# Where streamed and stationary operands begin in memory: a float32 decoder on one core

## The chip, the cores and the metric

The kernel runs on one core of a Trainium2 chip. The core has a matrix engine, TensorE (PE in the profile; its weight loads are listed apart, as PEld), two engines for elementwise work, VectorE (DVE) and ScalarE (ACT), a small helper, GpSimd (POOL), and queues that move data from the chip's main memory, HBM, into the on-chip memory, SBUF. SBUF has 128 partitions; a tile has a row in each. TensorE takes two operands from SBUF: the *stationary* one, 128 columns that a weight load puts into the array, and the *streamed* one, up to 512 columns that then pass through it. The products are summed in a third memory, PSUM.

The metric is the time of one execution in microseconds (us), the median of several.

## The reference

Two decoder layers and a final norm, on 256 tokens of width 1024, in float32:

```python
for l in range(DEPTH):                       # 2
    h = rmsnorm(x, norm1[l])
    hq, hf, hi, hg, aq, ak, av, ga, gb = split_cols(h @ w_in[l])     # 1024 -> 7680 columns
    o_hg = hgrn2_chunked(silu(hq), 1 - f, hi, log(f))               # f from sigmoid(hf); 8 heads of 128
    y_a = (rmsnorm(o_hg, hg_norm[l]) * silu(hg)) @ w_pa[l]
    y_b = swa_with_sinks(rope(aq), rope(ak), av, attn_sinks[l]) @ w_pb[l]   # window 128, 16 / 4 heads of 64
    x = x + (sigmoid(ga) * y_a + sigmoid(gb) * y_b) @ w_o[l]
    h2 = rmsnorm(x, norm2[l])
    x = x + (silu(h2 @ w_gate[l]) * (h2 @ w_up[l])) @ w_down[l]     # hidden width 2816
return rmsnorm(x, final_norm)
```

The weights of the two layers are about 159 MB and are read once.

## The kernel before

**Three products for one.** TensorE's quick float32 mode rounds its operands, so each operand is split into a rounded high part and a rest, and three of the four cross products are summed. For a weight tile `raw` from HBM, ScalarE rounds it into `wh` and VectorE subtracts to get `wl` (function `ahead`, 300 pairs of 128 x 1024 elements). The activations are split in the same way, into `xh` and `xl`, `ah` and `al`, and so on.

**Two forms.** In form A (`form_a`, `down`) the activations are stationary, 128 tokens at a time, and the weights are streamed, 512 columns at a time: `ah` with `wh`, `ah` with `wl`, `al` with `wh`. The products `akv`, `aq`, `v`, `gate`, `gb`, `ga`, `yb`, `ya`, `wo` and `acc` (the product with `w_down`) are of this form, with 2160 streams of 512 columns in all. In form B (`form_b`) the weights are stationary, 128 columns at a time, and the activations are streamed. There `xx` holds the high and the low part side by side, 256 tokens each:

```python
self.xx = hp.tile([P, KT, 2, S], F32R, tag="xx", name=f"xx_{name}")
T.matmul(ps, wh[:, k, :], n.xx[:, k], start=k == 0, stop=k == KT - 1)               # wide: 512 columns
T.matmul(ps[:, 0:S], wl[:, k, :], n.xx[:, k, 0, :], start=False, stop=False)        # narrow: 256 columns
```

So a *wide* stream takes `wh` against both parts, and a *narrow* one `wl` against the high part. They come four and four: wide, narrow, narrow, wide, for the eight k tiles of a product. `pb` (the columns for `hf` and `hq`), `pg` (`w_gate`) and `pu` (`w_up`) are of this form. `pb` streams the activations of the first norm, `n1`, whose tile is also the stationary operand of `akv`, `aq`, `v`, `gate`, `gb` and `ga`; `pg` and `pu` stream those of the second norm, `n2`, which nothing else uses.

Every stream has a weight load of its own, of 128 columns, and the load for the next stream goes on beside the one that runs.

**Order.** The large products run one after the other on TensorE, in the order `akv`, `aq`, `v`, `pb`, `gate`, `gb`, `yb`, `ga`, `ya`, `wo`, and then groups of `pg`, `pu` and `acc`. The small products of attention and of the recurrence (`qk`, `pt`, `pv`, `lb`, `lv`, `lc`, `o`, ...) are side work, put between them by generators. The weights run ahead of their use: three raw tiles and five pairs of `wh` and `wl` are held, and ScalarE and VectorE refill a pair when TensorE is through with it.

**Where the tiles lie.** Within a partition, every tile that TensorE reads begins at a multiple of 64 bytes, and a row of 512, 256 or 128 elements of 4 bytes is a multiple of 64 too. So both operands of each of its instructions begin there.

All engine calls go through one helper, so that the profile puts them on line 55 and tells them apart by their tiles (`out<-in`).

Of the kernel before, what the change touches and what calls it, by code (L numbers as in the profile page):

```python
# [8 lines left out]
F32R = mybir.dt.float32r  # L9
# [6 lines left out]
P = 128  # L16
D = 1024
S = 256
NT = S // P
DEPTH = 2  # L20
KT = D // P
# [6 lines left out]
EPS = 1e-6  # L28
MIN_F = 1e-30
NRAW, NW = 3, 5  # L30
YA, YB, YC, YS, YO, YP, YD, YE, YQ = 4, 3, 4, 2, 2, 2, 3, 2, 5
NEG = -1e30

# [7 lines left out]
def trunk(ctx, tc, x, norm1, w_in, lb_logits, hg_norm, attn_sinks, w_pa, w_pb, w_o, norm2,  # L41
# [4 lines left out]
    class Ordered:  # L46
        def __init__(self, engine):
            self.engine = engine
            self.always = engine is nc.tensor
# [11 lines left out]

    hp = ctx.enter_context(tc.tile_pool(name="hp", bufs=1))
    hp.tile([P, 224], F32, tag="lead", name="lead")
    hp.tile([P, KT, 2, S], F32R, tag="xx", name="xx_lead")
    st = hp.tile([P, 8, P], F32, tag="st", name="st")
    cp = ctx.enter_context(tc.tile_pool(name="cp", bufs=1))
    rawp = ctx.enter_context(tc.tile_pool(name="rawp", bufs=NRAW))
    wp = ctx.enter_context(tc.tile_pool(name="wp", bufs=NW))
# [34 lines left out]
    g2, ghg, lbl = (gcol[:, i, 0] for i in range(3))  # L103
# [56 lines left out]
                plan += [(w_down[l], groups[gi - 1][0], 4, 512 * c, 512) for c in range(2)]  # L160
        plan.append((w_down[l], groups[-1][0], 2, 0, D))

    raws, ready = [], []
    taken = [0]

    def load(j):
        src, k0, nk, c0, n = plan[j]
        raw = rawp.tile([P, nk, n], F32, tag="raw", name=f"raw{j}")
        step_ = nk // 2 if j < 2 else nk
        for k in range(0, nk, step_):  # L170
            nc.sync.dma_start(raw[:, k:k + step_], src[(k0 + k) * P:(k0 + k + step_) * P, c0:c0 + n].rearrange(
                "(k p) c -> p k c", p=P))
        if j == 0:
            nc.sync.dma_start(xs[1], x[0, P:2 * P, :])
        elif j == 1:
            nc.sync.dma_start(cf, const_f)
            G.memset(rows, 0.0)
            for i, vec in enumerate((norm2, hg_norm, lb_logits)):
                nc.scalar.dma_start(rows[32 * i:32 * i + 16, :], vec.rearrange("l (k p) -> (l k) p", p=P))
            nc.scalar.dma_start(nsink, attn_sinks.rearrange("l h -> (l h)").partition_broadcast(P))  # L180
        if nk == KT:
            parts = [raw[:, :, i * P:(i + 1) * P] for i in range(n // P)]
        elif n == 512:
            parts = [raw[:, 2 * i:2 * i + 2, :] for i in range(nk // 2)]
        else:
            parts = [raw[:, i:i + 1, :] for i in range(nk)]
        raws.extend(parts)
# [3 lines left out]
    def ahead(n):  # L191
        while len(ready) < min(n, 2 * len(plan)):
            while loaded[0] < len(plan) and len(raws) < len(ready) + 4:
                load(loaded[0])
                loaded[0] += 1
            i = len(ready)
            shape = list(raws[i].shape)
            hi = wp.tile(shape, F32R, tag="wh", name=f"wh{i}")
            lo = wp.tile(shape, F32R, tag="wl", name=f"wl{i}")
            A.copy(hi, raws[i])  # L200
            V.tensor_tensor(lo, raws[i], hi.bitcast(F32), ALU.subtract)
            ready.append((hi, lo))

    def take(n):
        i = taken[0]
        ahead(i + max(n, NW - 1))
        taken[0] += n
        return ready[i:i + n]

    def used():  # L210
        done[0] += 1
        ahead(done[0] + NW - 1)
# [65 lines left out]
        A.activation(dst, ps, AF.Copy, scale=r)  # L278

    class Norm:  # L280
        def __init__(self, gain, name):
            self.gain, self.name = gain, name
            self.xx = hp.tile([P, KT, 2, S], F32R, tag="xx", name=f"xx_{name}")
            self.xh, self.xl = self.xx[:, :, 0, :], self.xx[:, :, 1, :]
            self.rb = sm.tile([P, 1, S], F32, tag="rb", name=f"rb_{name}", bufs=1)
            self.ss = sm.tile([P, NT, 3], F32, tag="ss", name=f"ss_{name}")
            self.r = [sm.tile([P, 1], F32, tag=f"r{t}", name=f"r_{name}{t}") for t in range(NT)]
# [79 lines left out]
    def layer(l, n1):  # L367
# [422 lines left out]
        for _ in it:  # L790
            pass

        n2 = Norm(g2[:, l], f"n2_{l}")
        parts = []

        def put_x(c):
# [132 lines left out]
    nx = Norm(g1[:, 0], "n1_0")  # L929
    nx.turn(0, 0)  # L930
    ahead(1)
    nx.turn(0, 1)
    ahead(2)
# [19 lines left out]
    for l in range(DEPTH):  # L953
        hold = []

        def whole():
            hold.append((yield from layer(l, nx)))

        run(whole())
        nx = hold[0]  # L960
# [53 lines left out]
```

## Time and profile before

| what | before |
|---|---|
| median of 3 runs | 948.55 us (948.11 to 948.85) |
| the profiled execution | 948.29 us, of it 946.6 us from the first to the last instruction |
| granted TensorE clock, mean | 0.997 |
| TensorE busy, matmuls | 931.1 us in 5706 |
| TensorE weight loads | 777.8 us in 5706 |
| VectorE, ScalarE busy | 678.4 us, 538.0 us |
| DMA | 161.13 MB, 170 GB/s |

A group row of the profile gives line, engine, operation and tiles, the shapes, the count, the busy time in us and the mean duration of one in ns, then the engine's idle time just before them and what ended it. A matmul's duration runs from its start to a modelled end, which lies well behind the next one's start, since the matmuls are pipelined. What a matmul takes from TensorE's time is the distance to the next start, and this is read from the pieces of the chain of waits, or from starts in the timeline.

### The profile page before, as it was taken

The numbers are of one execution on the slowest core, as the hardware profiler recorded it, in microseconds if no ns is written. First come the engines' busy times: TensorE is split into PE (matmuls) and PEld (weight loads), VectorE is DVE, ScalarE is ACT, GpSimd is POOL, SyncE is SP. The second block draws the span as 40 slices with busy tenths as digits, with TensorE's granted clock in tenths as the row PEclk, the third lists the DMA queues.
The fourth block names the chain that finished last, engine by engine and source line by source line (L and its number), as shares of the span: only waits on it lengthen the run. The fifth ranks groups of instructions, "written<-read, shape, count | busy, mean of one in ns | idle before, by whom it ended". The sixth has DMA issues, their size and how long they took to land.

```text
span 946.6 us, 14348 instructions
## 1 busy us (share of the span) xinstructions
PE 931.1 (98%) x5706; PEld 777.8 (82%) x5706; DVE 678.4 (72%) x1176; ACT 538.0 (57%) x914; POOL 16.4 (2%) x28
## 2 busy tenths in 40 slices
PE   7999999999999999999999999999999999999996
PEld 5878887888888888888878888878788888888885
DVE  6567879976677867766585677898857787667664
ACT  6556596545446555554465776955454555455543
POOL 1000000000000000000000000000000000000000
PEclk9999999999999999999999999999999999999998
DMA  7645454444455566556466444554445566556541
GB/s 284 224 129 176 142 167 138 168 144 153 159 176 179 179 188 207 183 180 201 152 201 200 134 134 134 178 179 135 144 157 180 166 198 200 180 180 203 195 135 45
DMA packets 110932, 161.13 MB, mean 170 GB/s; under 512 B 2769, under 2 KB 64401, under 8 KB 110865
## 3 DMA queue, kind: packets, MB, share of 16 engines
q1 hardware_dynamic: 110160, 159.12, 51.7%
q10 hardware_dynamic: 704, 1.10, 0.3%
q8 instruction: 45, 0.74, 0.3%
q14 instruction: 23, 0.18, 0.1%
HBM read 159.15 MB, written 1.05 MB: 169 GB/s over the span
## 4 chain that ended last, share of the span: by engine, by line
PE 94%; ACT 2%; DVE 2%; DMA 0%; issue 0%; POOL 0%; POOLq 0%; ACTq 0%; SPq 0%
PE pg L55 13%; PE pu L55 13%; PE acc L55 12%; PE pb L55 8%; PE yb L55 5%; PE ga L55 5%; PE gb L55 5%; PE gate L55 5%; PE wo L55 5%; PE ya L55 5%; PE aq L55 5%; PE v L55 4%; PE akv L55 2%; PE qk L55 1%; PE o L55 1%; PE pv L55 1%
## 5 line engine op out<-in xcount | busy, mean ns | idle before, releaser
L55 DVE TENSOR_TENSOR wl<-raw,wh 128x1024 fp32r<-128x1024 f32 x300 | 365.8, 1223 | 146.2 <-ACT wh L55 144.4
L55 ACT CAST wh<-raw 128x1024 fp32r<-128x1024 f32 x300 | 314.9, 1053 | 203.6 <-PE acc L55 61.3
L55 PE MATMUL pu<-xx_n,wh 128*128 128x512 f32 x352 | 92.6, 393 | 0.0
L55 PE MATMUL pg<-xx_n,wh 128*128 128x512 f32 x352 | 92.5, 393 | 0.0
L55 PEld LDWEIGHTS pg<-xx_n,wh 128*128 128x128 f32 x352 | 63.2, 189 | 10.9
L55 PEld LDWEIGHTS pu<-xx_n,wh 128*128 128x128 f32 x352 | 63.1, 189 | 10.9
L55 PE MATMUL acc<-wl,ah 128*128 128x512 f32 x176 | 69.0, 392 | 0.0
L55 PE MATMUL acc<-wh,al 128*128 128x512 f32 x176 | 68.8, 391 | 0.0
L55 PE MATMUL acc<-wh,ah 128*128 128x512 f32 x176 | 68.2, 391 | 0.0
L55 PE MATMUL pb<-xx_n,wh 128*128 128x512 f32 x256 | 67.3, 397 | 0.0
L55 PEld LDWEIGHTS pb<-xx_n,wh 128*128 128x128 f32 x256 | 45.1, 189 | 8.8 <-issue 1.0
L55 PEld LDWEIGHTS pu<-xx_n,wl 128*128 128x128 f32 x352 | 48.4, 190 | 3.6
L55 PEld LDWEIGHTS pg<-xx_n,wl 128*128 128x128 f32 x352 | 48.1, 190 | 3.9 <-ACT xx_n L55 0.6
L55 PE MATMUL pg<-xx_n,wl 128*128 128x256 f32 x352 | 50.1, 284 | 0.0
L55 PE MATMUL pu<-xx_n,wl 128*128 128x256 f32 x352 | 49.7, 282 | 0.0
L55 ACT COPY zg<-pg 128x256 f32<-128x256 f32 x44 | 16.4, 373 | 54.1 <-PE pg L55 54.1
L55 PE MATMUL ga<-wh,xx_n 128*128 128x512 f32 x128 | 43.7, 402 | 0.0
L55 PE MATMUL gb<-wh,xx_n 128*128 128x512 f32 x128 | 43.1, 400 | 0.0
L55 PE MATMUL v<-wh,xx_n 128*128 128x512 f32 x128 | 41.2, 395 | 0.0
L55 PE MATMUL gate<-wh,xx_n 128*128 128x512 f32 x128 | 40.9, 394 | 0.0
L55 PE MATMUL aq<-wh,xx_n 128*128 128x512 f32 x128 | 40.3, 391 | 0.0
L55 ACT ACTIVATE sp<-sp,stat 128x128 f32<-128x128 f32 (+1 forms) x64 | 28.3, 443 | 19.8 <-DVE stat L55 19.8
(221 smaller groups left out, 1671.7 us busy)
## 6 DMA issues: line engine op xcount, KB each, us to landing
raw<-in_w_in SPq DMA_DIRECT2D x58, 1024.0 KB, 5.2
raw<-in_w_gate SPq DMA_DIRECT2D x22, 1024.0 KB, 5.1
raw<-in_w_up SPq DMA_DIRECT2D x22, 1024.0 KB, 5.2
raw<-in_w_down SPq DMA_DIRECT2D x22, 1024.0 KB, 5.0
raw<-in_w_pb SPq DMA_DIRECT2D x8, 1024.0 KB, 5.0
raw<-in_w_pa SPq DMA_DIRECT2D x8, 1024.0 KB, 5.2
raw<-in_w_o SPq DMA_DIRECT2D x8, 1024.0 KB, 4.9
raw<-in_w_in SPq DMA_DIRECT2D x4, 512.0 KB, 6.2
```

The lines of the kernel that those rows point to most:

```text
L55: ins = call(*args, **kw)
```

## The change

A constant, `SHIFT = 8` elements, or 32 bytes. The room of a weight tile is longer by 16 elements (64 bytes). A weight tile that is streamed (rows of 512 or 1024 columns) begins 8 elements into its room, one that is stationary (128 columns) at its beginning. The two parts of the activations of a norm each get 16 elements more, so that they are no longer side by side but 64 bytes apart; those of `n2` are put 8 elements in, and those of `n1` at the beginning. A wide stream of form B thereby reads two runs of 256 columns, with the gap between them left out. The tiles behind these rooms move up, by multiples of 64 bytes.

After this, the streamed operands of form A and of `pg` and `pu` begin 32 bytes behind a multiple of 64, and all their stationary operands on one. `pb` and the small products keep both on multiples of 64. The instructions of each engine and their order stay as they are.

```diff
+SHIFT = 8
...
-    hp.tile([P, KT, 2, S], F32R, tag="xx", name="xx_lead")
+    hp.tile([P, KT, 2, S + 2 * SHIFT], F32R, tag="xx", name="xx_lead")
...
     def ahead(n):
...
-            shape = list(raws[i].shape)
-            hi = wp.tile(shape, F32R, tag="wh", name=f"wh{i}")
-            lo = wp.tile(shape, F32R, tag="wl", name=f"wl{i}")
+            nk, cols = raws[i].shape[1:]
+            o = 0 if cols == P else SHIFT
+            rooms.append([wp.tile([P, nk * cols + 2 * SHIFT], F32R, tag=f"w{c}", name=f"w{c}{i}") for c in "hl"])
+            hi, lo = (room[:, o:o + nk * cols].rearrange("p (k c) -> p k c", k=nk) for room in rooms[-1])
             A.copy(hi, raws[i])
             V.tensor_tensor(lo, raws[i], hi.bitcast(F32), ALU.subtract)
...
     class Norm:
-        def __init__(self, gain, name):
+        def __init__(self, gain, name, shift=0):
             self.gain, self.name = gain, name
-            self.xx = hp.tile([P, KT, 2, S], F32R, tag="xx", name=f"xx_{name}")
+            self.room = hp.tile([P, KT, 2, S + 2 * SHIFT], F32R, tag="xx", name=f"xx_{name}")
+            self.xx = self.room[:, :, :, shift:shift + S]
             self.xh, self.xl = self.xx[:, :, 0, :], self.xx[:, :, 1, :]
...
-        n2 = Norm(g2[:, l], f"n2_{l}")
+        n2 = Norm(g2[:, l], f"n2_{l}", SHIFT)
```

More of the change, by code (lines that the diff above doesn't have):

```diff
@@ L161, in trunk @@
         plan.append((w_down[l], groups[-1][0], 2, 0, D))
-    raws, ready = [], []
+    raws, ready, rooms = [], [], []
     taken = [0]
```

## The prediction

> **What bounds the kernel now.** I read the page's busy shares first, then who waited for whom on TensorE, then the chain of waits piece by piece, and last the single instructions. The first row is the busy time of each engine, the second the granted clock in 40 slices, the third the chain that ended last.
>
> ```profile
> PE 931.1 (98%) x5706; PEld 777.8 (82%) x5706; DVE 678.4 (72%) x1176; ACT 538.0 (57%) x914; POOL 16.4 (2%) x28
> PEclk9999999999999999999999999999999999999998
> PE 94%; ACT 2%; DVE 2%; DMA 0%; issue 0%; POOL 0%; POOLq 0%; ACTq 0%; SPq 0%
> ```
>
> TensorE is busy nearly all the time at its full clock, and it makes up 94% of the chain. These are all the waits that it has (total us, times, longest):
>
> ```profile
> PE gps L55 <- DMA rows<-in_norm: 3.9, 1, 3.9
> PE akv L55 <- ACT xx_n L55: 1.7, 3, 0.9
> PE akv L55 <- DVE wl L55: 1.1, 1, 1.1
> PE rp_n L55 <- DVE dg_n L55: 0.7, 1, 0.7
> PE xp_n L55 <- DMA x<-in_x: 0.5, 1, 0.5
> PE qp L55 <- DVE att0l L55: 0.2, 1, 0.2
> ```
>
> That is 8.1 us, most of it at the start. So the time is the sum of the spacings from one matmul's start to the next, and a change of addresses can move it only through those spacings. The chain's pieces give them (start, length in us, instructions in a row):
>
> ```profile
> 29.32 16.38 PE aq L55 x72
> 45.78 8.22 PE v L55 x36
> 94.58 5.78 PE pb L55 x32
> 131.84 6.82 PE gate L55 x30
> 247.29 14.11 PE ya L55 x62
> 274.31 6.84 PE wo L55 x30
> 302.64 5.59 PE pg L55 x32
> 308.22 5.59 PE pu L55 x32
> 336.16 10.88 PE acc L55 x48
> ```
>
> The `acc` piece holds 48 streams of 512 columns in 10.88 us: 226.7 ns each. The `pg` piece holds 16 streams of 512 columns and 16 of 256. At the pace of `acc` these would take 16 x 226.7 + 16 x 113.3 ns = 5.44 us; they take 5.59. So there are two paces in this kernel for the same amount of data. Single instructions show where they part:
>
> ```profile
> 315.51 2.00 PE L55 MATMUL pg<-xx_n,wh 128*128 128x512 f32 x8
> 317.35 1.12 PE L55 MATMUL pg<-xx_n,wl 128*128 128x256 f32 x8
> 318.30 1.09 PE L55 MATMUL pg<-xx_n,wh 128*128 128x512 f32 x4
> 319.23 0.62 PE L55 MATMUL pu<-xx_n,wh 128*128 128x512 f32 x2
> L55 PE MATMUL pg<-xx_n,wl x352: 277/283/387, 291.0 to 915.6; 128*128 128x256 f32 x176
> L55 PE MATMUL acc<-wh,ah x176: 388/390/477, 336.0 to 938.4; 128*128 128x512 f32 x176
> L55 PEld LDWEIGHTS pg<-xx_n,wh x352: 186/188/193, 289.9 to 916.2; 128*128 128x128 f32 x176
> L55 PEld LDWEIGHTS pg<-xx_n,wl x352: 186/192/193, 290.8 to 915.5; 128*128 128x128 f32 x176
> ```
>
> From the starts: eight narrow streams take 318.30 - 317.35 = 0.95 us, 118.8 ns each, 5.5 over the 113.3. Eight wide ones take 317.35 - 315.51 = 1.84 us, 230.0 ns each, 3.3 over; the four behind the narrow ones take 0.93 us, 232.5 each, 5.8 over. The last four rows are durations of one instruction, shortest, median and longest in ns (a stream's holds some 164 ns behind the next one's start). Most narrow streams last 283 ns and the quickest 277, so the quick pace occurs here too. And the weight loads that belong to narrow streams last 192 ns where those of wide ones last 188: load and stream are slow together. I read this as the two colliding in their reads of the same memory, at some starting phases and not at others.
>
> **The change part by part.** It adds and removes no instruction, and on each engine the instructions stand in the same order with the same waits as before. Only addresses move, in four ways.
>
> First, `n2`'s activations, streamed in `pg` and `pu`, begin 32 bytes behind a multiple of 64, while the weights loaded for them stay on one. If the offset takes the stream out of the load's phase, the excess of these pieces goes: 0.15 us for 32 instructions, and 4 x 352 = 1408 of them make 44 such pieces, so 6.6 us. The eight-by-eight count above gives the same from single rows: 8 x 5.5 + 8 x 3.3 = 70 ns for 16, 6.2 us for all.
>
> Second, the weights that are streamed in form A (`akv`, `aq`, `v`, `gate`, `gb`, `ga`, `yb`, `ya`, `wo`, `acc`) begin 32 bytes behind as well. `acc`, with 3 x 176 = 528 streams, has nothing to give, as it runs at 226.7 already. The other pieces quoted, `aq`, `v`, `gate`, `ya` and `wo`, hold 230 streams in 16.38 + 8.22 + 6.82 + 14.11 + 6.84 = 52.37 us, 227.7 ns each, 1.0 over. By the code, `akv` has 96 streams and each of the other eight products 2 layers x 2 chunks x 8 k tiles x 2 token tiles x 3 = 192, together 1632, so 1.6 us. These pieces are undisturbed ones; behind the small products of the side work I expect a little more, and leave it out.
>
> Third, the two halves of an activation row are now 64 bytes apart, so a wide stream of `pg`, `pu` and `pb` reads two runs of 256 columns instead of one of 512. The nearest row is two narrow streams: at the quick pace they take 2 x 113.3 = 226.6 ns, as one wide one does, so that even a break between two instructions costs nothing there. I take 0. `pb` gets this break and nothing else: its activations are also stationary in form A and stay on a multiple of 64. Its pieces (5.78 us) should not move.
>
> Fourth, ScalarE writes `wh`, and VectorE reads it and writes `wl`, at the shifted addresses.
>
> ```profile
> L55 DVE TENSOR_TENSOR wl<-raw,wh 128x1024 fp32r<-128x1024 f32 x300 | 365.8, 1223 | 146.2 <-ACT wh L55 144.4
> L55 ACT CAST wh<-raw 128x1024 fp32r<-128x1024 f32 x300 | 314.9, 1053 | 203.6 <-PE acc L55 61.3
> ```
>
> Both wait for others by the rows' last columns, ScalarE for TensorE to give buffers back. 300 pairs in 946.6 us are one per 3.16 us, against 1.05 and 1.22 us of work. I take 0. Without that cover each percent would cost 300 x 12 ns = 3.7 us on VectorE. A TensorE that is 1% faster does not outrun them either, as VectorE has 268 us free and the only wait for `wl` is 1.1 us at the start.
>
> What the trace cannot show is the price of the new phase, as before the change every stationary and every streamed operand begins on a multiple of 64. The bounds come from the rows. Below, the quickest thing of 128 columns that repeats here is a transpose with its load:
>
> ```profile
> 78.82 1.47 PE L55 MATMUL pt<-ident,sp 128*128 128x128 f32 x12
> L55 PE MATMUL pt<-ident,sp x96: 271/273/275, 78.8 to 604.1; 128*128 128x128 f32 x96
> ```
>
> Twelve last 1.47 us and one lasts 0.273, so eleven steps take 1.197 us, 109 ns each, and that is the load's pace. A narrow stream that needs a load cannot be quicker than 109, and a wide one at that pace would take 218. Above, the wide streams behind narrow ones, at 232.5 ns, are what a form A stream could become. Between these ends I take the quick pace of the same instructions in this trace, 226.7 and 113.3, for the shifted groups: it is what they show when load and stream do not meet.
>
> The sum: 6.6 + 1.6 = 8.2 us off the profiled execution's 948.29 us (span 946.6, and 1.7 around it) gives 940.1. The median of the runs is 948.55, 0.26 above that execution, so 940.3.
>
> One rule speaks against it. The Trainium skill, "TensorE: Matmul & The Clock Gate", step-by-step part on LDWEIGHTS, gives TensorE two independent SBUF read ports and says that loading the next weights takes no read bandwidth from the running matmul. By that the sum is 0 and the time stays. The rows above agree with it only in part: a load goes on beside every `acc` stream without a trace of it, but the narrow streams and their loads are slow together.
>
> **The rivals.**
>
> *Nothing moves (948.5, from 946.6 to 950.4).* The phase may not be set by the addresses at all, but by when a load starts against its stream. `acc`, at its quick pace with both operands on multiples of 64, speaks for this: if equal alignment alone made them meet, it would be slow. The narrow streams are the ones in which the load fills almost all of the time (109 of 113 ns), and this too could make them slow at any address. Against it stands that the quickest narrow streams, at 277 ns, have the same load beside them. The Trainium skill's rule of two ports leads here too.
>
> *Slower: form A loses its quick phase (953 to 959.5).* The place is the streams of weights, 2160 of them, now at 226.7 to 227.7 ns with both operands on a multiple of 64. If 32 bytes is the offset at which they meet, they go to the 232.5 of the slow wide rows: 528 x 5.8 + 1632 x 4.8 ns = 10.9 us. With `pg` and `pu` no better that is 948.55 + 10.9 = 959.5; with them cured, 952.9. Then it decides from 8.2 / (10.9 + 1.6) = 66% of the form A streams on; without the cure, from the first few. For it: these streams have little to win and more to lose, and a phase that is good in one form need not be in the other. Against it: after every disturbance form A comes back to its quick pace, so there it seems to find a good phase rather than have one by chance.
>
> *Much faster: the stream's own pace depends on its start (about 912).* 226.7 and 113.3 ns are proportional to the columns, so something slows the stream evenly, with or without a load beside it. If the start decides this and the pace goes to the 109 per 256 columns above, the shifted streams win another 704 x 4.3 + 2864 x 8.7 ns = 27.9 us (2864 = 704 + 2160), so 940.3 - 27.9 = 912.4. For it: the proportion. Against it: a stream crosses as many boundaries of 64 bytes from either start. The Trainium skill, "TensorE: Matmul & The Clock Gate", section "Back-to-back issue gap", gives 512 columns 216 ns for matmuls alone; no row here shows it, and by it a wide stream would win 10.7 instead of 8.7 ns.
>
> **How the numbers follow.** The forecast, collisions gone for all or most of the shifted streams and 2 to 12 us with them, gets 0.40, with a range of its own from 936 to 946. Nothing gets 0.22, slower 0.27, much faster 0.11. A difference of 0.2%, 1.9 us, is what a measurement here can tell from none. So faster 0.51, the same 0.22, slower 0.27. The predicted time is the forecast's, 940.3. For 8 in 10 the range runs from 922 to 957: it holds the forecast and no change whole, leaves most of the much faster case out below (0.09), and above about a third of the slower case (0.09), where form A loses and `pg` and `pu` are not cured.
>
> **What would show it.** Right: narrow streams of `pg` and `pu` at a median near 277 ns with loads at 188, pieces of 32 at 5.44 us, `aq` and `ya` near 226.7 ns a stream, and, as the control, `pb` still at 5.78. The first step is wrong if the narrow median stays at 283; the second, if the `acc` piece grows from 10.88 towards 48 x 232.5 = 11.16 us; the own-pace reading is ruled out if it stays at 10.88. If `pb` moves, the gap between the two halves counts and not the offset. Waits of TensorE on `wh` or `wl` would show that the other engines' shifted accesses have a price. The forecast falls as a whole if slow streams come just as often and merely in other groups.

## The result, and the profile after

The changed kernel takes 958.65 us (median of 5 runs, 958.25 to 959.42) against 948.55 us before: a ratio of 1.0109, with a 95% interval from 1.0097 to 1.0121. It is 10.1 us slower, where 8.2 us faster had been forecast, and above the range. The profiled execution spans 956.6 us against 946.6.

First the busy times of the changed kernel, then pieces of its chain of waits (start, length in us, instructions in a row).

```profile
PE 941.7 (98%) x5706; PEld 776.9 (81%) x5706; DVE 679.3 (71%) x1176; ACT 537.7 (56%) x914; POOL 16.5 (2%) x28
...
29.67 16.75 PE aq L56 x72
...
95.52 5.78 PE pb L56 x32
...
249.67 14.44 PE ya L56 x62
277.07 7.00 PE wo L56 x30
...
316.84 5.62 PE pg L56 x32
339.31 11.20 PE acc L56 x48
```

TensorE is busy for 10.6 us more, in as many instructions; VectorE, ScalarE and the weight loads are as before. The `acc` piece has gone from 10.88 to 11.20 us, from 226.7 to 233.3 ns a stream. `aq` (227.5 to 232.6 ns), `ya` and `wo` have grown by about 5 ns a stream. `pg` and `pu` pieces took 5.58 or 5.59 us and now take 5.60 to 5.63. The pieces of `pb`, the control, took 5.78 to 5.80 us and now scatter from 5.76 to 5.82.

Form B by single instructions: the timeline of one `pg` product, then durations (shortest, median, longest in ns) of its streams, of `acc`'s, and of its loads.

```profile
318.54 2.02 PE L56 MATMUL pg<-xx_n,wh 128*128 128x512 f32 x8
320.40 1.12 PE L56 MATMUL pg<-xx_n,wl 128*128 128x256 f32 x8
321.36 1.10 PE L56 MATMUL pg<-xx_n,wh 128*128 128x512 f32 x4
...
L56 PE MATMUL pg<-xx_n,wh x352: 388/395/483, 293.1 to 926.3; 128*128 128x512 f32 x176
L56 PE MATMUL pg<-xx_n,wl x352: 276/280/384, 294.1 to 925.5; 128*128 128x256 f32 x176
L56 PE MATMUL acc<-wh,ah x176: 388/394/484, 339.1 to 948.4; 128*128 128x512 f32 x176
L56 PEld LDWEIGHTS pg<-xx_n,wl x352: 186/188/194, 293.8 to 925.3; 128*128 128x128 f32 x176
```

The narrow streams have become a little quicker, 280 ns where they had 283, and their loads last 188 ns instead of 192. But the wide ones went from a median of 390 to 395, and eight of them now take 320.40 - 318.54 = 1.86 us instead of 1.84. The narrow ones' gain is too small for a single product: in this one eight take 321.36 - 320.40 = 0.96 us, where those of before took 0.95. It shows in the sum. Added up over all streams in the two traces, each from its start to the next one's, form A costs 8.8 us more (the expectations below have 8.9; it hangs on how the borders between groups are counted), `pg` and `pu` 1.0 more (narrow streams -0.9, wide ones +1.9), `pb` less than 0.1 and the small products 0.1. That is the whole 10.0 us of the span. Within `pb`, narrow streams gained 0.2 us and wide ones lost 0.3.

### The profile page after: what moved, and what is told of

Read it like the earlier page. It is cut to its first block, busy times and chain, and to the rows that moved or that the text cites. A ratio compares the mean times of both kernels' runs of the same rounds, so it can differ in the third digit from the quotient of the medians.

```text
span 956.6 us, 14348 instructions
## 1 busy us (share of the span) xinstructions
PE 941.7 (98%) x5706; PEld 776.9 (81%) x5706; DVE 679.3 (71%) x1176; ACT 537.7 (56%) x914; POOL 16.5 (2%) x28
## 4 chain that ended last, share of the span: by engine, by line
PE 95%; DVE 2%; ACT 2%; DMA 0%; issue 0%; POOL 0%; POOLq 0%; ACTq 0%; SPq 0%
PE pg L56 13%; PE pu L56 13%; PE acc L56 12%; PE pb L56 8%; PE yb L56 5%; PE ga L56 5%; PE gb L56 5%; PE gate L56 5%; PE wo L56 5%; PE aq L56 5%; PE ya L56 5%; PE v L56 4%; PE akv L56 2%; PE qk L56 1%; PE o L56 1%; PE pv L56 1%
## 5 line engine op out<-in xcount | busy, mean ns | idle before, releaser
L56 PEld LDWEIGHTS acc<-wl,ah 128*128 128x128 f32 x176 | 33.0, 188 | 8.6 <-DVE wl L56 0.9
```

The lines of the kernel that those rows point to most:

```text
L56: ins = call(*args, **kw)
```

## The experiments

Two theories stood at first. **A**: what counts is where a stream begins against the load that runs beside it. **B**: a stream that does not begin on a multiple of 64 pays, whatever the load does. Three of the runs are a small kernel that computes something else, chains of matmuls that differ in their addresses only; all others are the decoder with its whole computation. Each of the small kernels was executed once. *Settled* below means the mean spacing at a chain's end, over its last 24 streams or its last sets.

### Chains with different starts

Rounded data in two tiles, one streamed and one loaded; for each pair of starts, 48 matmuls in a row:

```diff
+            a = 512 * (i % 8) + s4
+            b = 128 * (i % 8) + l4
+            keep(nc.tensor.matmul(ps[0:c, 0:n], stat[:, b:b + c], strm[:, a:a + n], start=i == 0, stop=i == REP - 1))
```

Here `s4` and `l4` are the two starts in elements of 4 bytes, and the rows are 512 elements (2048 bytes) and 128 (512 bytes) long.

> A separate small kernel, not the decoder: 33 chains of 48 matmuls with a weight load each, on rounded float32 data and with nothing running beside them, in which only the starting bytes of the stream (s) and of the load (l), the stream's columns and the load's columns differ; its output is a few columns of the products and not the decoder's. Theory A (the phase between load and stream decides): spacing depends on s - l alone. s0 l0, s64 l0, s0 l64, s128 l0, s16 l16 and s32 l32 are at 226.7 ns, s32 l0 and s0 l32 at about 233; with loads of 64 and 32 columns the excess at s32 falls to about a half and a quarter of the 6.6 ns. Theory B (a stream that does not begin on a multiple of 64 pays, whatever the load): s32 l32 and s16 l16 are as slow as s32 l0, s0 l32 is at 226.7, and the excess is the same for loads of 128, 64 and 32 columns. Theory C (it needs the decoder's other traffic or its wide and narrow order): all chains of 512 columns at 226.7. For 256 columns, where the decoder has 118.8 ns at s0, all three leave the best offset open; by A some offset should reach 113.3.

Pieces of the chain of waits of this kernel. A name holds the bytes of the stream's start (s), of the load's (l) and the load's columns (c); pieces under 6 us have streams of 256 columns, the others of 512.

```profile
71.75 11.20 PE s32B_l0B_c128w L50 x48
116.42 11.01 PE s64B_l0B_c128w L50 x48
...
161.04 11.19 PE s0B_l32B_c128w L50 x48
183.42 11.20 PE s0B_l64B_c128w L50 x48
194.62 10.93 PE s32B_l32B_c128w L50 x48
205.55 11.10 PE s16B_l16B_c128w L50 x48
216.65 5.75 PE s0B_l0B_c128w L50 x48
228.16 5.60 PE s16B_l0B_c128w L50 x48
239.51 5.61 PE s32B_l0B_c128w L50 x48
273.74 11.04 PE s0B_l0B_c64w L50 x48
284.78 11.09 PE s32B_l0B_c64w L50 x48
295.88 11.11 PE s0B_l0B_c32w L50 x48
318.16 10.93 PE s0B_l0B_c128w L50 x48
```

With nothing running beside them, the chains show both paces of the decoder. Equal starts at 0 or at 32 give 10.93 us, and their settled streams 226.7 ns. A stream 32 bytes off its load, in either direction, gives 11.2 us and 233.3 to 233.4 ns. Theory B falls: 32 and 32 is quick although the stream is off its multiple of 64, and 0 and 32 is slow although it is on it. Theory C of the expectation, that the decoder's other traffic is needed, falls as well. Two things that theory A had expected failed too. Differences of 64 and 128 bytes are slow as well (a stream 64 bytes up, at 228.9 ns, the least so), so the phase does not count by 64; and equal starts at 16 are slow (231.1 ns settled). Nor did the excess fall with the load's columns: with loads of 64 and 32 columns s32 l0 is near s0 l0, as expected of a smaller excess, but only because s0 l0 has lost its quick pace (11.04 and 11.11 us).

Narrow streams take 120.0 ns at s0 l0, near the decoder's 118.8, and 116.7 at s16 or s32. No start tried reached 113.3.

### Both operands 32 bytes up

```diff
-    hp.tile([P, 224], F32, tag="lead", name="lead")
+    hp.tile([P, 232], F32, tag="lead", name="lead")
```

> The kernel before with 32 bytes more ahead of the first tile, so that streamed and stationary operands alike begin 32 bytes behind a multiple of 64. Theory A (relative phase): nothing changes, 948.5 us within 1, acc pieces of 48 at 10.88 us. Theory B (the stream's own start): as slow as the change or slower, since pb and the small products pay as well: 958.7 to 961 us, acc pieces near 11.2.

948.5 us, ratio 1.0 (0.9991 to 1.001); the chain's pieces are those of before:

```profile
30.06 16.36 PE aq L55 x72
303.34 5.59 PE pg L55 x32
336.86 10.88 PE acc L55 x48
```

So in the decoder, too, it is not the multiple of 64 that counts but the place of stream and load against each other.

### The two halves of the change apart

Only the streamed weights shifted, in their rooms of 4160 bytes, the norms as before:

> Only the streamed weights of form A are shifted by 32 bytes; the norms' activations are as before. If the parts add up, by the sums of spacings in the two traces (form A +8.9 us): 957.4 us, pg pieces back at 5.59 us, acc pieces at 11.2. If a slow form A comes from form B's phase being carried over, less than half of it.

958.28 us, ratio 1.01 (1.0084 to 1.0115). `acc` pieces are at 11.2 us. The `pg` pieces do not come back to 5.59 but scatter a little (5.58 to 5.61 in the first group): the longer rooms move their stationary weights too, by 64 bytes from room to room.

```profile
306.25 5.61 PE pg L56 x32
...
328.64 5.58 PE pg L56 x32
339.83 11.22 PE acc L56 x48
```

Only the norms' activations changed, the weights as before:

> Only the norms' activations are changed (64 bytes between the parts, those of the second norm 32 bytes behind a multiple of 64); the streamed weights are as before. If the parts add up: +1.0 us in pg and pu, 949.6 us, acc pieces at 10.88. By the prediction's first step, which the trace of the change speaks against, -6.6 us: 941.9.

952.43 us, ratio 1.0039 (1.0025 to 1.0053): 3.8 us slower, where adding the parts gave 1.0. `acc` is back at 10.88, but the products of the first norm have become slower, `aq` from 16.38 to 16.52 us a piece, although nothing of the first norm is shifted by 32 bytes. The halves cost 9.6 and 3.8 us alone and 10.1 together, so both slow the same streams: `aq` and the four products that share its loads lose 4.5 us with the weights' half, 2.7 with the norms' and 4.0 with both. Once a stream is off its load's phase, a second reason adds nothing.

```profile
29.58 16.52 PE aq L56 x72
304.01 5.61 PE pg L56 x32
337.69 10.88 PE acc L56 x48
```

This made a new question. Before the change, the operands of the large products lay not just on multiples of 64 from each other, but on multiples of 512. Which of the two is needed?

### By how many bytes does the phase count?

Again chains, the wide ones now led in by 12 streams at s0 l0:

> The small kernel of chains again, not the decoder, its tiles on multiples of 1024 bytes. Names: kind (w 40 wide streams, r 12 wide ones at s0 l0 to start each chain alike, n 40 narrow ones, b four wide and then five times eight narrow and eight wide), stream's start, load's start. Theory A64 (the phase counts by 64 bytes): every w chain with s - l a multiple of 64 is at 226.7 ns. Theory A512 (it counts by 512 bytes, the length of a load, or more): s512 l0, s0 l512, s1024 l0, s64 l64, s128 l128 are at 226.7 and s64 to s384 against l0 at 229 to 233.5. The equal pairs at 4, 8 and 48 bytes: 226.7 by either, if only the difference counts; the first run's 231.1 for 16 and 16 speaks against that for starts off a multiple of 32. Narrow chains: 116.7 to 120. b chains tell which pair would be best for form B: s0 l0 as in the decoder, 8 + 8 in 2.80 us; a pair under 2.76 would be worth a try.

Pieces of this kernel's chain; w are 40 wide streams, b are four wide and then five times eight narrow and eight wide, in the order of form B.

```profile
37.28 9.32 PE ws128B_l0B L55 x40
...
61.41 9.07 PE ws256B_l0B L55 x40
85.26 9.07 PE ws512B_l0B L55 x40
...
108.83 9.33 PE ws0B_l64B L55 x40
...
132.97 9.07 PE ws0B_l256B L55 x40
...
156.55 9.55 PE ws4B_l4B L55 x40
...
192.93 9.11 PE ws64B_l64B L55 x40
...
266.79 14.89 PE bs0B_l0B L55 x84
386.14 14.71 PE bs0B_l16B L55 x84
```

The phase counts by 256 bytes: differences of 256, 512 and 1024 run at 226.7 ns (9.07 us for 40), 128, 192 and 384 at 233.3 (232.3 with the load, and not the stream, 128 bytes up). The theory with 512 had the right idea and the wrong size. Equal starts at 64 and 128 are quick, those at 4, 8 and 48 bytes are not (239.2, 233.4 and 231.1 ns settled).

For form B, where narrow and wide streams alternate, s0 l0 is not the best: a load 16 bytes up takes 14.71 us for the same 84 streams. Its wide streams are at 226.7 ns there.

### The longer rooms alone, the gap alone, the 32 bytes alone

Every shift taken out, the weight rooms still 64 bytes longer, the norms as before:

```diff
-            o = 0 if cols == P else SHIFT
+            o = 0
```

> The longer rooms of the weight tiles (4160 bytes instead of 4096) without any shift of 32 bytes, the norms' activations as before: every operand is on a multiple of 64, but the streamed weights stand at all multiples of 64 against a grid of 512. Theory A64: nothing changes, 948.5 us. Theory A512: nine rooms of ten are out of phase, most of form A's +8.9 us comes back, 955 to 957 us, acc pieces 11.1 to 11.2.

956.18 us, ratio 1.008 (1.0063 to 1.0097), with `acc` at 11.11 to 11.14 us. Every operand lies on a multiple of 64, and three quarters of the change's loss is there.

```profile
338.74 11.11 PE acc L56 x48
```

If the ten rooms lie one behind the other, room i begins 64 x i bytes off, and only those at 0, 256 and 512 bytes stand at a multiple of 256 from their loads: seven of ten are out of phase (by 512 it would be eight, not the nine of the expectation). As an estimate, 10.88 + 0.7 x (11.20 - 10.88) = 11.10 us for the `acc` piece, close to the 11.11 to 11.14 measured. In the change itself all streamed weights are out of phase, which is why it costs more.

Only the gap between a norm's two parts, nothing shifted, weights as before:

> Only the 64 bytes between the two parts of the norms' activations, no shift: all operands on multiples of 64, but rows 1088 bytes apart instead of 1024. Theory A64: 948.5 us. Theory A512: the loads of the first norm's activations leave the grid, and aq, v, gate, gb and ga pay as they did with the norms' part of the change, +2.8 us, with up to +1 in form B: 951 to 952.5 us, ya, wo and acc pieces unchanged.

952.24 us, ratio 1.0037 (1.0023 to 1.005). `aq` takes 16.58 and 16.51 us a piece, `ya` is at 14.08 and `acc` at 10.92. These 3.5 us are nearly all of the 3.8 that the norms' half cost, so the second norm's 32 bytes add 0.3 us at most. By the sums of spacings, 2.6 us of it are form A, 0.8 `pg` and `pu` and 0.2 `pb`.

```profile
29.48 16.58 PE aq L56 x72
248.70 14.08 PE ya L56 x62
337.64 10.92 PE acc L56 x48
```

All weight tiles 32 bytes up as one block, rooms and norms as before:

> All weight tiles 32 bytes up in one block, with rooms of 4096 bytes as before and everything else on its old grid: the streams of form A are exactly 32 bytes against their loads, and so are the loads of form B against their streams. Both theories: form A at 233.3 ns, +8.9 us; form B, by the first run's chains, 1.7 ns less for each of 960 narrow and some 3 ns more for each of 960 wide streams, +1.3; together 958.7 us. If it stays under 952, 32 bytes alone are harmless and the longer rooms did the damage.

961.0 us, ratio 1.0129 (1.0114 to 1.0144), the slowest of all. `acc` is at 11.20, `aq` at 16.79 and `pg` at 5.61 to 5.63 us. The 32 bytes do the damage by themselves, without longer rooms.

```profile
29.81 16.79 PE aq L55 x72
306.47 5.63 PE pg L55 x32
```

It is 2.3 us over what was expected. By the sums of spacings most of that is form A, at +10.4 us instead of the 8.9 taken over from the changed kernel (the weights' half alone had +9.9); form B has +2.0 instead of the 1.3 that the chains gave.

Rooms longer by 256 bytes, no shift:

```diff
-SHIFT = 8
+SHIFT, ROOM = 0, 64
...
-            rooms.append([wp.tile([P, nk * cols + 2 * SHIFT], F32R, tag=f"w{c}", name=f"w{c}{i}") for c in "hl"])
+            rooms.append([wp.tile([P, nk * cols + ROOM], F32R, tag=f"w{c}", name=f"w{c}{i}") for c in "hl"])
```

> The rooms of the weight tiles longer by 256 bytes instead of 64, no shift: every stream stands at a multiple of 256 from its load, the norms' activations as before. If the phase counts by 256 bytes, as the chains of the last run say: 948.5 us, acc pieces of 48 at 10.88. If by 512 or 1024 in the decoder: half of the rooms or more out of phase, 953 or more.

948.43 us, ratio 0.9997 (0.9988 to 1.0006): the time of before, with every `acc` piece of 48 at 10.88 us. With 64 bytes the same step cost 7.5 us. So the decoder counts by 256 bytes as the chains do.

```profile
336.28 10.88 PE acc L56 x48
```

### A better start for form B

Chains of four wide and seven times eight narrow and eight wide streams, all streams from byte 0, over the starts of the wide loads (w) and of the narrow ones (n):

> The small kernel of chains, not the decoder: four wide and then seven times eight narrow and eight wide streams, all streams from byte 0, with the load of the wide ones (w) and of the narrow ones (n) at the bytes of the names. The decoder's pair w0 n0 should take 2.79 us for 8 + 8, as in the last run, and w16 n16 2.76. If what counts is the difference within 256 bytes, the list of equal pairs shows at which loads form B is quickest, and the unequal pairs whether the narrow streams can have their best (114.2 ns at 64) and the wide ones theirs (226.7 at 16) together: 8 x 114.2 + 8 x 226.7 = 2.73 us. If each stream's pace hangs on the phase that the one before left, no pair gets there and they scatter between 2.74 and 2.83.

```profile
97.83 20.31 PE w16B_n16B L48 x116
159.40 20.18 PE w28B_n28B L48 x116
```

Settled, a set of 8 + 8 takes 2.793 us at w0 n0, 2.760 at 16 and 16, and 2.747 at 28 and 28, the best of 47 pairs on average (192 and 192 changes between 2.735 and 2.778 from set to set). The narrow streams' best (114.0 ns, at 64 and 64) and the wide ones' (226.6, at 16 and 16) did not come together: each of the unequal pairs tried took 2.77 us or more. So a stream's pace hangs on its own start and on what ran before it, as the last of the expected outcomes says.

All of form B's weights 16 bytes up, in rooms longer by 256 bytes:

> The same rooms, and the stationary weights of form B alone 16 bytes up; streams of form A and the norms' activations as before. By the chains s0 l16 (2.760 us for 8 + 8 against 2.794 at s0 l0), 120 such sets in pb, pg and pu: -4.1 us, 944.4 us, with pg pieces at 5.52 instead of 5.59. If the decoder's interruptions and the change between forms spoil the phase: 948.5 within 1.

946.32 us, ratio 0.9976 (0.9966 to 0.9985): quicker than before by 2.4 us, a little over half of the 4.1. Most `pg` and `pu` pieces came to the 5.52 us expected, but six of forty, in a row at the beginning of the second layer's feed-forward part, are at 5.62, and `pb` got slower (5.78 to 5.82). So the decoder does not always find the pattern that the chains settle in.

```profile
94.82 5.82 PE pb L56 x32
302.85 5.52 PE pg L56 x32
```

Only the weights of `pg` and `pu`, 28 bytes up (`ffn` marks the tiles of `w_gate` and `w_up`; the lines with - are those of the run just told):

```diff
-SHIFT, ROOM = 4, 64
+SHIFT, ROOM = 7, 64
...
-            o = SHIFT if cols == P else 0
+            o = SHIFT if ffn[i] else 0
```

> Rooms longer by 256 bytes, everything on its grid as before except the stationary weights of pg and pu, 28 bytes up; pb stays on the grid, as its pieces got slower with 16 bytes. By the chains (2.747 us for 8 + 8 at w28 n28 against 2.793 at w0 n0), a piece of 32 goes from 5.59 to 5.49 us, 44 of them: -4.1 us, 944.6 us, pb, aq, ya and acc pieces as before. If what the chains show at 28 bytes does not carry over: pieces of pg at 5.52 or more and 946 us or more.

944.64 us, ratio 0.9958 (0.9944 to 0.9971), 3.7 us quicker than the kernel before, of the 4.1 expected. That the time itself is the 944.6 us expected is in part luck, as the kernel before took 948.35 us beside this run. The pieces of `pg` and `pu` are all at the 5.49 us that the chains had said.

```profile
94.62 5.78 PE pb L56 x32
302.66 5.49 PE pg L56 x32
335.62 10.88 PE acc L56 x48
```

## Why the prediction was wrong

**What bounds the kernel** held: TensorE's spacings alone moved, its waits stayed as they were, and the other engines' shifted accesses cost nothing (VectorE 678.4 to 679.3 us).

**Two paces** held, and so did reading them as load and stream that get in each other's way at some phases: in chains with nothing else running, addresses alone switch between 226.7 and 233.3 ns. That rules out "nothing moves".

**The step that failed** is the choice of the price, "I take the quick pace of the same instructions in this trace, 226.7 and 113.3, for the shifted groups: it is what they show when load and stream do not meet". That pace belongs to one relation of the two addresses, and the change left that relation. Wide streams pay about 233.3 ns at most others. The text had this price as its upper end, at 232.5. It had also noted that `acc` was quick with equal starts, and used this only as an argument for no change, when it was a warning that the quick phase was the one to be lost.

**First**, `n2` out of phase, forecast at -6.6 us: `pg` and `pu` came to +1.0. The narrow streams did gain, as forecast in kind, with their loads at 188 ns, but 0.9 us and not the 88 x 8 x 5.5 ns = 3.9 us counted; the wide ones lost 1.9.

**Second**, form A, forecast at -1.6 us: it came to +8.8, and this is most of the result.

**Third**, the gap, "I take 0": alone it costs 3.5 us. The row it was priced by, two narrow streams in place of a wide one, speaks of the break in the stream. Most of the price was elsewhere: rows 1088 bytes apart take the same tile's loads in `aq`, `v`, `gate`, `gb` and `ga` off the phase, and these lost 2.7 us. Form B lost 1.0; whether by the break or by the new starts of its rows was not tested apart. For `pb` the zero came out in the change as a whole, but as a sum of a gain and a loss, and with the gap alone its pieces reached 5.83 us. Nor was `pb` the control it was taken for, with "this break and nothing else": the longer rooms move its loads by steps of 64 bytes too.

**A part that was not priced at all** is the longer room of the weight tiles: 64 bytes more, put down as moving tiles "by multiples of 64 bytes". That alone cost 7.5 us. The working took the layout of before for "multiples of 64", where by the code it was one on multiples of 512.

**The rivals.** The slower one named the place, the streams of form A, and its 959.5 us with `pg` and `pu` not cured is 0.9 us off. In part that is luck: its 10.9 us for form A came to 8.8, and `pg` and `pu`, held at 0, cost 1.0. Nor was its condition right, that 32 bytes is the offset at which load and stream meet: 64 bytes do it as well. It had been given 0.27, and its upper end was left outside of the range. Its argument against itself, that form A finds back to its quick pace after every disturbance, holds only where the difference of addresses allows that pace. "Much faster" is out: no chain of 512 columns, at any start tried, settled under 226.6 ns.

**The rule of two ports.** The Trainium skill, "TensorE: Matmul & The Clock Gate", step-by-step part on LDWEIGHTS, has the next load take no read bandwidth from the running matmul. Read as saying that a load cannot slow the matmul beside it, this does not hold in these runs with their rounded float32 operands: moving the load's start alone by 64 bytes takes 40 of them from 9.07 to 9.33 us (s0 l64 in the second run of chains, where s0 l256 has 9.07).

**What stays open** is the mechanism below the addresses: why the phase counts by 256 bytes, why equal starts must be on a multiple of 32, why narrow streams settle at 114 ns on average at best, and why 28 bytes suit a mixed order. The first two were measured over the starts listed and nothing else. Which memory resource the two share was not shown.

## What to carry to other kernels

Where TensorE is the bound, the distance between the starts of a streamed operand and of the one loaded beside it is a parameter that was worth 1 to 3% of the streams' time here. For the streams of 512 columns here it wants to be a multiple of 256 bytes with both on multiples of 32, so every pad between their tiles or rows should be one too, and a pad of 64 bytes is a change to be timed; the mixed order of form B did best elsewhere, at 28 bytes. A chain of some fifty matmuls per pair of addresses, all in one small kernel, shows the pace of each pair in a single run; its order of wide and narrow streams has to be that of the real kernel. Before pricing a new state, ask what is special about the old one: a layout that looks like "multiples of 64" may be one of 512.

## What the runs showed of the hardware that was not expected

- Wide streams with loads of 128 columns settle at 226.7 ns when the starts differ by a multiple of 256 bytes, both on multiples of 32, and at about 233.3 ns for most other pairs: the loss is much the same for nearly every wrong distance. The exceptions lie between, such as 228.9 at s64 l0, 230.0 at s48 l0 and 231.1 for equal starts at 16, and above: 235.0 at s4 l0, and 239.2 for equal starts at 4.
- Narrower loads do not help: with equal starts at 0, loads of 64 and 32 columns gave 11.04 and 11.11 us for 48 wide streams, slower than the 10.93 of 128 columns.
- A settled pattern depends on what ran before: the same eight wide streams take 226.7 ns each in a chain of their own and 230.1 behind eight narrow ones.
